# Two sums of a weight block made by an accumulating DMA, one more seven-product pair in gate/up, and the feed-forward stage in three parts

## The chip, the cores and the metric

The kernel runs on one core of one Trainium2 chip. A core has five engines that run their own instruction streams: TensorE (PE in the profile; PEld is its weight load), VectorE (DVE), ScalarE (ACT), GpSimd (POOL) and SyncE (SP, used here only to issue DMAs). Sixteen DMA engines move data between device memory (HBM) and the on-chip memory SBUF; PSUM holds the accumulators of TensorE. The metric is the device time of one execution in microseconds; smaller is better.

## The reference

A decoder trunk of two layers on 256 tokens of width 2048, in float32. Each layer has an input projection, three kinds of mixers in parallel, an output projection, and then the feed-forward stage (FFN), which this change is about:

```python
h = rms_norm(x, norm_ffn_w[l])
x = x + (jax.nn.silu(h @ ffn_w_gate[l]) * (h @ ffn_w_up[l])) @ ffn_w_down[l]
```

`ffn_w_gate` and `ffn_w_up` are 2048 x 5632, `ffn_w_down` is 5632 x 2048, for each of the two layers. The rest of the trunk is left as it is.

## The kernel before

**Precision.** Each float32 operand is split in a high part, rounded by ACT (`wh = Copy(raw)`, line 316), and a low part, made by DVE (`wl = raw - wh`, line 317). A product is then three matmuls into the same accumulator: high times high, low times high, high times low (line 1309, in `prod`).

**Tiles.** The FFN weights come in tiles `raw` of 128 x 1024, 512 KB, of which five are in flight (`RAW = 5`). Two tiles make a pair `kp`, which covers 256 rows of the contraction and two columns of 512: a 2 x 2 block of weights, against the 2 x 2 block of activations of the same 256 rows and the two halves of the 256 tokens. The layout of the weights in HBM is made beforehand (`_pairs`).

**Two kinds of pair.** A plain pair (kind `c`) does eight block products, 24 matmuls of 512 columns. A seven-product pair (kinds `s0`, `s1`, `s2`, in the manner of Strassen and Winograd) does seven, 21 matmuls, and has to make sums of blocks first. The sums of activations, four of 128 x 128, are made in `block_sums`: for gate/up on POOL, once a layer; for down on DVE, when a gate_up has ended, in `finish`. The sums of weights are made by DVE in `split`, lines 338 to 341: with raw = [a, b] of the first tile and r1 = [c, d] of the second, each 128 x 512, line 338 makes u1 = [a + d, b + d] in one instruction, line 340 a + d + b, line 341 that plus c, both in u2. Lines 344 and 345 split c; raw, u1 and u2 are then split as any tile. `SEVEN = (2, 4, 5)` names the seven-product pairs among the 8 of gate/up, `DOWN_SEVEN` six among the 22 of down.

**Loops.** `ffn` goes through the 11 column groups f of 512 in parts (`FFN_PARTS = [6, 5]`). In each part it calls `gate_up(f)` for each f, and then `down(g2)` for the two halves of the output columns, over the pairs 2f and 2f+1 of these f. `down` adds its result to the residual `res`: eight DVE adds around the seven-product terms (in `mid`) and four at the end. More parts mean more calls of `down`, and fewer activations held at a time. The very last group (layer 1, last part, second half) goes through `dense` and `final`, with plain tiles (`wdown`). What a gate_up leaves to be done late (its transposes, `finish`) is issued after the first pair of the next call (`flush`).

**Order and queues.** The code calls `wtile` for each part. It lets `fetch` issue loads so far that five tiles are loaded ahead of what has been split, on SP's DMA queue, and lets `split` run two parts ahead of TensorE (`SPLIT = 3` buffers). A framework turns the code into one instruction stream for each engine, may reorder instructions within a stream, and puts in the semaphore waits. Each stream then runs in order. The pool `up` has 22 buffers of 128 x 1040, for all working tiles `u`: activations, sums, and whatever else the stage holds.

Of the kernel before, what the change touches and what calls it, by code (L numbers as in the profile page):

```python
# [10 lines left out]
ALU = mybir.AluOpType  # L11
PSUM = bass.MemoryType.PSUM

P = 128
# [7 lines left out]
RWKV_EPS = 64e-5  # L22
EXP_HALF = math.exp(-0.5)

FFN_PARTS = [6, 5]

SEVEN = (2, 4, 5)

DOWN_SEVEN = (2, 5, 8, 14, 17, 19)

# [27 lines left out]
class Trunk:  # L60
# [194 lines left out]
    def plan(self):  # L255
        seq, parts, done = [], [], []

        def plain(tiles, kind="n"):
            for t in tiles:
                parts.append((kind, len(seq)))  # L260
                seq.append(t)
                done.append(len(seq))

        def pairs(w, first, kps, seven):
            for kp in kps:
                t = [(w, (first + 2 * kp + j) * P * 1024, 512) for j in range(2)]
                if kp in seven:
                    parts.extend((f"s{j}", len(seq)) for j in range(3))
                    seq.extend(t)
                    done.extend([len(seq)] * 3)  # L270
                else:
                    plain(t, "c")
        for l in range(DEPTH):
            off = 0
            for n in (IN_W[name] for name in IN_ORDER):
                plain((f"win{l}", off + kp * 2 * P * n, n) for kp in range(8))
                off += D * n
            for g in range(4):
                plain(("wout", (l * 4 + g) * D * 512 + kp * 2 * P * 512, 512) for kp in range(8))
            f0 = 0  # L280
            for nf in FFN_PARTS:
                for f in range(f0, f0 + nf):
                    pairs("wgu", (l * 11 + f) * 16, range(8), SEVEN)
                lastp = f0 + nf == 11
                for g2 in range(2):
                    if lastp and l + 1 == DEPTH and g2:
                        for g in range(2):
                            plain(("wdown", g * 2 * nf * 2 * P * 512 + kp * 2 * P * 512, 512) for kp in range(2 * nf))
                    else:
                        pairs("wdp", (l * 2 + g2) * 44, range(2 * f0, 2 * (f0 + nf)), DOWN_SEVEN)  # L290
                f0 += nf
        self.seq, self.parts, self.done = seq, parts, done
        self.loaded, self.cast, self.used = [], [], 0

    @staticmethod
    def cuts(i, n):
# [3 lines left out]
    def fetch(self, upto):  # L300
        while len(self.loaded) < min(upto, len(self.seq)):
            w, off, n = self.seq[len(self.loaded)]
            raw = self.wp.tile([P, 1024], F32, tag="raw", name=self.nm("raw"), bufs=self.RAW)
            src = self.A[w][off:off + 2 * P * n].rearrange("(p f) -> p f", p=P)
            for c in self.cuts(len(self.loaded), n):
                self.nc.sync.dma_start(raw[:, c], src[:, c])
            self.loaded.append(raw)

    def split(self, upto):
        nc = self.nc  # L310

        def halve(raw, cuts):
            wh = self.wp.tile([P, 1024], F32R, tag="wh", name=self.nm("wh"), bufs=self.SPLIT)
            wl = self.wp.tile([P, 1024], F32R, tag="wl", name=self.nm("wl"), bufs=self.SPLIT)
            for c in cuts:
                nc.scalar.activation(wh[:, c], raw[:, c], AF.Copy)  # L316
                nc.vector.tensor_tensor(wl[:, c], raw[:, c], wh[:, c].bitcast(F32), op=ALU.subtract)  # L317
            return wh, wl
        while len(self.cast) < min(upto, len(self.parts)):
            p = len(self.cast)  # L320
            kind, i = self.parts[p]
            raw = self.loaded[i]
            if kind == "n" and i >= len(self.seq) - 2 * FFN_PARTS[-1]:
                wh, wl = self.U(F32R), self.U(F32R)
                nc.scalar.activation(wh[:, :1024], raw, AF.Copy)
                nc.vector.tensor_tensor(wl[:, :1024], raw, wh[:, :1024].bitcast(F32), op=ALU.subtract)
                self.cast.append((wh, wl))
            elif kind == "n":
                self.cast.append(halve(raw, self.cuts(i, self.seq[i][2])))
            elif kind == "c":  # L330
                self.cast.append(halve(raw, [slice(0, 1024)]))
            elif kind == "s0":

                r1 = self.loaded[i + 1]
                u1, u2 = self.U(), self.U()
                h = lambda t, j: t[:, j * 512:(j + 1) * 512]
                v = lambda t: t[:, :1024].rearrange("p (a c) -> p a c", a=2)
                nc.vector.tensor_tensor(v(u1), v(raw), h(r1, 1).rearrange("p (o c) -> p o c", o=1).to_broadcast([P, 2, 512]),  # L338
                                        op=ALU.add)
                nc.vector.tensor_tensor(h(u2, 0), h(u1, 0), h(raw, 1), op=ALU.add)  # L340
                nc.vector.tensor_tensor(h(u2, 1), h(u2, 0), h(r1, 0), op=ALU.add)
                wh, wl = halve(raw, [slice(0, 1024)])
                b = self.U(F32R)
                nc.scalar.activation(h(b, 0), h(r1, 0), AF.Copy)
                nc.vector.tensor_tensor(h(b, 1), h(r1, 0), h(b, 0).bitcast(F32), op=ALU.subtract)
                self.cast.append((wh, wl, b))
                self.sums = (u1, u2)
                self.loaded[i + 1] = None
            else:
                self.cast.append(halve(self.sums[int(kind[1]) - 1][:, :1024], [slice(0, 1024)]))  # L350
            self.loaded[i] = None
# [81 lines left out]
    def post_pair(self, kp, src, scale, xh, xl):  # L433
# [10 lines left out]
        self.tt(fl(xl), w[:, :512], fl(xh).bitcast(F32), ALU.subtract)  # L444
        if kp in SEVEN:
            self.comb[kp] = self.block_sums(w, "pool")
# [905 lines left out]
    def gate_up(self, f, rstd):  # L1352
# [19 lines left out]
        def finish(t):  # L1372
            ps = self.PS()
            for k in range(4):
                self.tr(ps[:, k * P:(k + 1) * P], sg[:, t * 512 + k * P:t * 512 + (k + 1) * P], self.ident)
            o, p4 = hh[:, :, t * P:(t + 1) * P], ps.rearrange("p (k c) -> p k c", k=4)
            self.act(o, p4, AF.Copy)
            self.tt(hl[:, :, t * P:(t + 1) * P], p4, o.bitcast(F32), ALU.subtract)
            for b in need:

                self.act(need[b][:, 0:512].rearrange("p (k s c) -> p k s c", k=2, s=2)[:, :, t, :],
                         p4[:, 2 * b:2 * b + 2, :], AF.Copy)
                if t:
                    self.hcomb[2 * f + b] = self.block_sums(need[b], "dve")
        need = {b: self.U() for b in range(2) if 2 * f + b in DOWN_SEVEN}
        self.late += [lambda: finish(0), lambda: finish(1)]
        return hh, hl

    def ffn(self, l):
        f0 = 0  # L1390
        xt, rstd = self.xt, self.rstd
        for pi, nf in enumerate(FFN_PARTS):
            self.hcomb = {}
            hts = [self.gate_up(f, rstd) for f in range(f0, f0 + nf)]
            lastp = pi == len(FFN_PARTS) - 1

# [145 lines left out]
def _tiles(w, n):  # L1542

    k = w.shape[0] // (2 * P)
    return np.ascontiguousarray(w.reshape(k, 2, P, n).transpose(0, 2, 1, 3)).reshape(-1)


def _pairs(a, b, seven):

    k = a.shape[0] // (2 * P)  # L1550
    w = np.stack([a.reshape(k, 2, P, 512), b.reshape(k, 2, P, 512)], axis=2).transpose(0, 1, 3, 2, 4)
    o = np.empty((k, 2, P, 2, 512), w.dtype)
    for kp in range(k):
        if kp in seven:
            o[kp, 0, :, 0], o[kp, 0, :, 1], o[kp, 1, :, 0], o[kp, 1, :, 1] = \
                w[kp, 0, :, 0], w[kp, 1, :, 1], w[kp, 1, :, 0], w[kp, 0, :, 1]
        else:
            o[kp] = w[kp]
    return o.reshape(-1)


def _layout(i):
# [54 lines left out]
    for l in range(DEPTH):  # L1617
# [3 lines left out]
        wo += [_tiles(w[:, g * 512:(g + 1) * 512], 512) for g in range(4)]  # L1621
        gu += [_pairs(i["ffn_w_gate"][l][:, g * 512:(g + 1) * 512], i["ffn_w_up"][l][:, g * 512:(g + 1) * 512], SEVEN)
               for g in range(11)]
        d = [i["ffn_w_down"][l][:, g * 512:(g + 1) * 512] for g in range(4)]
        dp += [_pairs(d[2 * g], d[2 * g + 1], DOWN_SEVEN) for g in range(2)]
        if l + 1 == DEPTH:
            down += [_tiles(d[g][-512 * FFN_PARTS[-1]:], 512) for g in (2, 3)]
    o["wout"], o["wgu"], o["wdp"], o["wdown"] = (np.concatenate(x) for x in (wo, gu, dp, down))
# [23 lines left out]
```

## Time and profile before

| | us |
|---|---|
| median of 3 runs | 2401.75 (2401.61 to 2407.05) |
| profiled execution | 2401.77 |
| its span, first to last instruction | 2400.0 |
| DVE: first operation of a seven-product pair, line 338 | 106.1, 87 times |
| DVE: low parts from raw tiles, line 317 | 866.3, 720 times |
| DMA moved | 436.04 MB, mean 182 GB/s |

An "f period" below is the time between the same instruction in two gate_up calls that follow each other. A row of instructions by group has the line, the engine, the operation, out <- in, shapes and count, then the busy time and the mean duration in ns, and then the time that the engine idled before them and what ended it. A row of a timeline has the start, the duration, the engine, the line, the operation and in brackets the idle time before it. `u`, `raw`, `wh`, `wl`, `xh`, `xl`, `res` are tiles of the program; `dn` and `mx` are accumulators in PSUM.

### The profile page before, as it was taken

To read this page: it belongs to the slowest core of one execution; us is meant where nothing else is said; L and a number is where in the kernel's file an instruction comes from. 1 tells how busy PE (TensorE), PEld (TensorE's weight loads), DVE (VectorE), ACT (ScalarE), POOL (GpSimd) and SP (SyncE) were. 2 spreads that over 40 slices of the span, in tenths; PEclk is the share of its full clock that TensorE was granted. 3 is DMA by queue.
4 is the path that set the end of the run, shared out by engine and by line. 5 is a ranking of instruction groups with operands and counts; after the bars stand their busy time and mean duration, and the time that the engine had idled before them with its cause. 6 is when DMAs were issued, how large, how long until landed. Compare 5 with 4: busy or idle time off the path is not lost.

```text
span 2400.0 us, 34089 instructions
## 1 busy us (share of the span) xinstructions
PE 2374.5 (99%) x12947; PEld 1994.1 (83%) x12947; DVE 1874.1 (78%) x2439; ACT 1312.9 (55%) x1761; POOL 119.8 (5%) x149
## 2 busy tenths in 40 slices
PE   8999999999999999999999999999999999999998
PEld 8998888788888888778799988887878888887786
DVE  7777656589898788998867866565888987889884
ACT  6445755555555455555554547555555554555553
POOL 3100110100000000000001101101000000000000
PEclk9999999999999999999999999999999999999999
DMA  8464554555656565565644544545555565556654
GB/s 292 147 172 112 158 164 151 184 187 194 197 188 204 189 206 195 177 199 192 210 152 150 167 118 157 164 160 182 189 192 190 193 211 188 198 193 186 222 189 149
DMA packets 139429, 436.04 MB, mean 182 GB/s; under 512 B 30464, under 2 KB 30720, under 8 KB 139264
## 3 DMA queue, kind: packets, MB, share of 16 engines
q1 hardware_dynamic: 137360, 428.52, 55.2%
q0 software_dynamic: 1184, 4.19, 0.5%
q8 instruction: 101, 1.65, 0.3%
q10 hardware_dynamic: 720, 1.15, 0.2%
q14 instruction: 64, 0.52, 0.1%
HBM read 430.66 MB, written 3.15 MB: 181 GB/s over the span
## 4 chain that ended last, share of the span: by engine, by line
PE 87%; DVE 6%; ACT 3%; DMA 2%; issue 2%; POOL 0%; ACTq 0%; SPq 0%; POOLq 0%; DVEq 0%
PE dn L1309 41%; PE mx L1309 9%; PE dn L401 6%; PE dn L399 6%; PE dn L400 6%; PE dn L391 4%; PE dn L393 4%; PE dn L392 4%; PE mx L131 4%; DVE wl L317 2%; ACT wh L316 2%; PE mx L135 2%; DVE u L105 2%; ACT u L123 1%; DVE u L338 1%
## 5 line engine op out<-in xcount | busy, mean ns | idle before, releaser
L316 ACT ACTIVATE wh<-raw 128x1024 fp32r<-128x1024 f32 (+3 forms) x720 | 740.8, 1038 | 651.6 <-PE dn L1309 264.0
L317 DVE TENSOR_TENSOR wl<-raw,wh 128x1024 fp32r<-128x1024 f32 (+3 forms) x720 | 866.3, 1211 | 284.5 <-ACT wh L316 277.9
L1309 PE MATMUL dn<-wh,xh 128*128 128x512 f32 x946 | 372.0, 393 | 0.0
L1309 PE MATMUL dn<-wh,xl 128*128 128x512 f32 x946 | 368.9, 390 | 0.0
L1309 PE MATMUL dn<-wl,xh 128*128 128x512 f32 x946 | 365.0, 390 | 0.0
L1309 PE MATMUL dn<-wh,u 128*128 128x512 f32 x1128 | 352.4, 394 | 0.0
L316 ACT ACTIVATE wh<-u 128x1024 fp32r<-128x1024 f32 x174 | 184.7, 1062 | 215.2 <-PE dn L1309 100.3
L391 PE MATMUL dn<-xh,wh 128*128 128x256 f32 x896 | 258.3, 289 | 7.4 <-ACT wh L316 7.4
L393 PE MATMUL dn<-xh,wl 128*128 128x256 f32 x896 | 254.5, 286 | 1.2 <-DVE wl L317 1.1
L392 PE MATMUL dn<-xl,wh 128*128 128x256 f32 x896 | 255.0, 285 | 0.0
L317 DVE TENSOR_TENSOR wl<-u,wh 128x1024 fp32r<-128x1024 f32 x174 | 211.5, 1222 | 53.9 <-ACT wh L316 53.8
L1309 PEld LDWEIGHTS dn<-wh,u 128*128 128x128 f32 x1128 | 211.1, 188 | 48.1 <-DVE u L105 0.8
L1309 PE MATMUL dn<-wl,u 128*128 128x512 f32 x564 | 220.8, 394 | 0.1
L1309 PEld LDWEIGHTS dn<-wh,xh 128*128 128x128 f32 x946 | 177.6, 188 | 42.5 <-DVE u L105 3.9
L1309 PEld LDWEIGHTS dn<-wl,xh 128*128 128x128 f32 x946 | 177.6, 188 | 37.6
L1309 PEld LDWEIGHTS dn<-wh,xl 128*128 128x128 f32 x946 | 177.7, 188 | 35.9
L1309 PE MATMUL mx<-wh,u 128*128 128x512 f32 x564 | 180.8, 398 | 0.9
L391 PEld LDWEIGHTS dn<-xh,wh 128*128 128x128 f32 x896 | 173.4, 193 | 9.9 <-ACT wh L316 7.6
L393 PEld LDWEIGHTS dn<-xh,wl 128*128 128x128 f32 x896 | 172.9, 194 | 2.0 <-DVE wl L317 1.8
L392 PEld LDWEIGHTS dn<-xl,wh 128*128 128x128 f32 x896 | 173.5, 194 | 0.1
L399 PE MATMUL dn<-wh,xh 128*128 128x512 f32 (+2 forms) x448 | 170.4, 380 | 0.0
L401 PE MATMUL dn<-wl,xh 128*128 128x512 f32 (+2 forms) x448 | 162.4, 366 | 1.2 <-DVE wl L317 1.1
(179 smaller groups left out, 3482.9 us busy)
## 6 DMA issues: line engine op xcount, KB each, us to landing
raw<-wgu SPq DMA_DIRECT2D x352, 512.0 KB, 3.6
raw<-win SPq DMA_DIRECT2D x175, 512.0 KB, 4.0
raw<-wdp SPq DMA_DIRECT2D x156, 512.0 KB, 4.2
raw<-wout SPq DMA_DIRECT2D x64, 512.0 KB, 4.2
raw<-win SPq DMA_DIRECT2D x32, 340.0 KB, 3.0
raw<-wdown SPq DMA_DIRECT2D x20, 512.0 KB, 4.3
raw<-win SPq DMA_DIRECT2D x16, 360.0 KB, 3.1
u<-xt SPq DMA_DIRECT2D x8, 256.0 KB, 7.2
```

Source lines behind the costliest of these rows:

```text
L105: self.nc.vector.tensor_tensor(out, a, b, op=op)
L131: self.nc.tensor.matmul(out, lhsT=lhsT, rhs=rhs, start=start, stop=stop)
L135: self.nc.tensor.transpose(out, in_, ident)
L316: nc.scalar.activation(wh[:, c], raw[:, c], AF.Copy)
L317: nc.vector.tensor_tensor(wl[:, c], raw[:, c], wh[:, c].bitcast(F32), op=ALU.subtract)
L391: nc.tensor.matmul(o, lhsT=wh[:, c], rhs=xh, start=st and m % 2 == 0, stop=False)
L392: nc.tensor.matmul(o, lhsT=wh[:, c], rhs=xl, start=False, stop=False)
L393: nc.tensor.matmul(o, lhsT=wl[:, c], rhs=xh, start=False, stop=sp and m % 2 == 1)
L399: nc.tensor.matmul(o, lhsT=xh[:, x], rhs=wh[:, c], start=st, stop=False)
L400: nc.tensor.matmul(o, lhsT=xl[:, x], rhs=wh[:, c], start=False, stop=False)
L401: nc.tensor.matmul(o, lhsT=xh[:, x], rhs=wl[:, c], start=False, stop=sp)
L1309: mm(o, lhsT=x[a], rhs=w[b], start=start and i == 0, stop=stop and i == 2)
```

## The change

Line 338 goes. Instead, for each seven-product pair, `fetch` loads the first tile a second time, into a buffer u1 of the pool `up` (on SP's queue, right behind the load of the tile itself), and has POOL's DMA queue add the block d to both halves of u1: a DMA with an accumulating add, whose source is the block d in HBM, read twice. It is issued as soon as the second copy is there. `split` takes the finished u1 from `self.early`.

With that, pair 6 of gate/up becomes a seven-product pair (four of 8), down has five such pairs of 22 at other places, and the FFN is done in three parts of 4, 4 and 3 column groups instead of two of 6 and 5.

```diff
-FFN_PARTS = [6, 5]
-
-SEVEN = (2, 4, 5)
-
-DOWN_SEVEN = (2, 5, 8, 14, 17, 19)
+FFN_PARTS = [4, 4, 3]
+
+SEVEN = (2, 4, 5, 6)
+
+DOWN_SEVEN = (2, 5, 10, 13, 18)
...
+        self.summed, self.early = {i for kind, i in parts if kind == "s0"}, {}
...
             for c in self.cuts(len(self.loaded), n):
                 self.nc.sync.dma_start(raw[:, c], src[:, c])
+            if len(self.loaded) in self.summed:
+
+                u1 = self.U()
+                self.nc.sync.dma_start(u1[:, :1024], src)
+                b12 = self.A[w][off + 2 * P * n:off + 4 * P * n].rearrange("(p o f) -> p o f", p=P, o=2)[:, 1:2, :]
+                self.nc.gpsimd.dma_start(u1[:, :1024].rearrange("p (o f) -> p o f", o=2), b12.to_broadcast([P, 2, n]),
+                                         accum_op=ALU.add)
+                self.early[len(self.loaded)] = u1
             self.loaded.append(raw)
...
-                u1, u2 = self.U(), self.U()
+                u1, u2 = self.early.pop(i), self.U()
                 h = lambda t, j: t[:, j * 512:(j + 1) * 512]
-                v = lambda t: t[:, :1024].rearrange("p (a c) -> p a c", a=2)
-                nc.vector.tensor_tensor(v(u1), v(raw), h(r1, 1).rearrange("p (o c) -> p o c", o=1).to_broadcast([P, 2, 512]),
-                                        op=ALU.add)
                 nc.vector.tensor_tensor(h(u2, 0), h(u1, 0), h(raw, 1), op=ALU.add)
                 nc.vector.tensor_tensor(h(u2, 1), h(u2, 0), h(r1, 0), op=ALU.add)
```

## The prediction, made before the changed kernel was run

> **What bounds the kernel now.** I read the page's head and busy shares first, then the windows of the feed-forward stage (FFN), then single instructions in the timelines. Windows rows give the length, the busy time and instruction count of PE, PEld, DVE, ACT and POOL, the granted clock, the DMA share and GB/s.
>
> ```profile
> span 2400.0 us, 34089 instructions
> PE 2374.5 (99%) x12947; PEld 1994.1 (83%) x12947; DVE 1874.1 (78%) x2439; ACT 1312.9 (55%) x1761; POOL 119.8 (5%) x149
> PE 87%; DVE 6%; ACT 3%; DMA 2%; issue 2%; POOL 0%; ACTq 0%; SPq 0%; POOLq 0%; DVEq 0%
> ...
> 480.00:740.00 260.00, 259.51 (x1147) 209.32 (x1147) 232.46 (x271) 150.05 (x177) 1.61 (x1) 1.00 0.60 194
> 740.00:870.00 130.00, 130.00 (x567) 105.48 (x566) 100.32 (x107) 63.43 (x67) 0.00 (x0) 1.00 0.58 195
> ```
>
> TensorE sets the pace (99%, and 87% of the chain that ended last). 480 to 740 is six gate_up calls of layer 0, and there DVE is busy 232.5 of 260 us: 0.89. 740 to 870 is two down calls, DVE at 0.77. So gate/up is where DVE has least room. Next, what one matmul costs, and how long each gate_up takes. These are timeline rows (start, us, engine, line, operation): two matmuls 14 apart in a full stretch, and the DVE add that begins when the last matmul of a gate_up's first accumulator ends.
>
> ```profile
> 717.47 0.39 PE L1309 MATMUL dn<-wh,xh 128*128 128x512 f32 x1
> 720.64 0.39 PE L1309 MATMUL dn<-wl,xh 128*128 128x512 f32 x1
> ...
> 522.98 0.69 DVE L105 TENSOR_TENSOR u<-u,dn 128x512 f32<-128x512 f32 x1 [1.31 <-PE dn L1309]
> 565.71 0.69 DVE L105 TENSOR_TENSOR u<-u,dn 128x512 f32<-128x512 f32 x1 [1.31 <-PE dn L1309]
> 609.54 0.69 DVE L105 TENSOR_TENSOR u<-u,dn 128x512 f32<-128x512 f32 x1 [1.31 <-PE dn L1309]
> 653.36 0.69 DVE L105 TENSOR_TENSOR u<-u,dn 128x512 f32<-128x512 f32 x1 [1.31 <-PE dn L1309]
> 696.08 0.69 DVE L105 TENSOR_TENSOR u<-u,dn 128x512 f32<-128x512 f32 x1 [1.31 <-PE dn L1309]
> 739.95 0.69 DVE L105 TENSOR_TENSOR u<-u,dn 128x512 f32<-128x512 f32 x1 [1.31 <-PE dn L1309]
> ```
>
> One matmul costs 3.17 / 14 = 0.2264 us, not the 0.39 it is shown with (they overlap). A gate_up has 3 seven-product pairs of 21 matmuls and 5 plain pairs of 24: 183, or 41.4 us. The periods are 42.73, 43.83, 43.82, 42.72 and 43.87 us. The long ones are those of f = 2, 3 and 5, which follow f = 1, 2 and 4: just those whose outputs need block sums for down's pairs 2, 5 and 8, done on DVE at the start of the next f. So **1.1 us of TensorE is lost in each gate_up that carries such sums**. The place is the first seven-product pair (DVE rows, then two PE rows 15 matmuls apart):
>
> ```profile
> 707.45 1.02 DVE L105 TENSOR_TENSOR u<-u 128x128 f32<-128x128 f32 x4 [0.45 <-ACT u L123]
> 708.39 1.22 DVE L338 TENSOR_TENSOR u<-raw,raw 128x1024 f32<-128x1024 f32 x1
> 710.13 0.69 DVE L340 TENSOR_TENSOR u<-u,raw 128x512 f32<-128x512 f32 x1
> 710.82 1.22 DVE L317 TENSOR_TENSOR wl<-u,wh 128x1024 fp32r<-128x1024 f32 x1
> ...
> 710.92 0.39 PE L1309 MATMUL dn<-wl,u 128*128 128x512 f32 x1
> 715.17 0.39 PE L1309 MATMUL dn<-wh,xl 128*128 128x512 f32 x1
> ```
>
> Fifteen matmuls should take 3.40 us and took 4.25: the block sums push L338, L338 pushes the halves of u1 and u2, and TensorE gets those late.
>
> **The change, part by part.** All against the profiled execution: 2401.77 us (span 2400.0 and 1.77 around it), as good as the median of 2401.75.
>
> *Matmuls.* Pair 6 of gate/up becomes a seven-product pair: 11 x 2 = 22 more. Down goes from 21 such pairs (6 in layer 0's two calls each, 6 and 3 in layer 1) to 19 (10, 5 and 4; the last group, now 6 kps, stays plain). Net 20 pairs, 3 matmuls each: 60 x 0.2264 = **-13.6 us**. TensorE is the pace, so this counts in full as long as DVE and the DMAs keep up.
>
> *DVE.* The durations are the group rows (count | busy, mean ns):
>
> ```profile
> L338 DVE TENSOR_TENSOR u<-raw,raw 128x1024 f32<-128x1024 f32 x87 | 106.1, 1220 | 11.6 <-DMA raw<-wgu 6.0 <-DMA raw<-wdp 5.4
> L340 DVE TENSOR_TENSOR u<-u,raw 128x512 f32<-128x512 f32 x87 | 59.8, 688 | 1.1
> L317 DVE TENSOR_TENSOR wl<-u,wh 128x1024 fp32r<-128x1024 f32 x174 | 211.5, 1222 | 53.9 <-ACT wh L316 53.8
> ```
>
> A seven-product pair costs DVE 1.22 (L338) + 3 x 0.69 + 3 x 1.22 = 6.95 us and now 5.73; a plain one 2.44. A gate_up had 3 x 6.95 + 5 x 2.44 = 33.1 and gets 4 x 5.73 + 4 x 2.44 = 32.7 us. So DVE's sum hardly changes, while TensorE's falls by 0.68: L338's time is spent on the fourth pair. What does change is the order at pair 2: u1 no longer waits for DVE, and everything behind L338 moves up 1.22, more than the 1.1 lost there. There are 6 such gate_ups a layer: 12 x 1.1 = **-13.2 us**, if u1 is there in time. The other end is 0 (the stall stays because ACT's and the remaining DVE steps are as late). What ACT gets more with the new pair, one conversion of a whole tile and one of a half, lies beside TensorE: ACT is at 150 of 260 us.
>
> *Three parts.* Each layer gets two more down calls; the last group in layer 1 stays plain, so 7 calls become 11. Each has 12 DVE adds of 0.69 us: 33 us more DVE work, in a stage where DVE had 30 of 130 us free, beside the plain pairs. What a call loses now:
>
> ```profile
> 805.51 0.69 DVE L105 TENSOR_TENSOR res<-res,dn 128x512 f32<-128x512 f32 x1 [1.34 <-PE dn L1309]
> 870.14 0.69 DVE L105 TENSOR_TENSOR res<-res,dn 128x512 f32<-128x512 f32 x1 [1.34 <-PE dn L1309]
> ```
>
> 64.63 us for 3 x 21 + 9 x 24 = 279 matmuls, 63.17 us: 1.5 lost. If it goes with the call, 4 more cost +5.8; if it goes with L338, up to 7 x 1.5 = 10 are won. I take 0 between these ends: 19 pairs for 21, with less DVE work each. The plain tail has 6 tiles a group for 10, the same matmuls in all; 0.
>
> *DMA.* Every seven-product pair (107 now) loads its first tile twice and has 512 KB added to the second copy by POOL's queue, from a 256 KB block read twice. The rows: the start of the kernel, where queues are full; queue rows; landings of loads and of POOL's own DMAs; and where the loads are issued.
>
> ```profile
> 10.00:25.00 15.00, 13.60 (x105) 13.19 (x104) 11.55 (x16) 13.04 (x21) 5.24 (x3) 1.00 1.03 409
> ...
> q1 hardware_dynamic: 137360, 428.52, 55.2%
> raw<-wgu SPq DMA_DIRECT2D x352, 512.0 KB, 3.6
> u<-rg POOLq DMA_DIRECT2D x2, 512.0 KB, 6.5
> u<-rm POOLq DMA_DIRECT2D x2, 512.0 KB, 3.8
> u<-fnw POOLq DMA_DIRECT2D x2, 512.0 KB, 6.6
> ...
> 1160.22 0.54 POOL L250 DMA_DIRECT2D u<-rg  x1 [0.85 <-PE mx L1309]
> ...
> 702.12 2.67 SPq L306 DMA_DIRECT2D raw<-wgu  x2
> 710.88 2.73 SPq L306 DMA_DIRECT2D raw<-wgu  x2
> 719.54 0.68 DVE L340 TENSOR_TENSOR u<-u,raw 128x512 f32<-128x512 f32 x1
> 724.75 0.68 DVE L340 TENSOR_TENSOR u<-u,raw 128x512 f32<-128x512 f32 x1
> ```
>
> At 409 GB/s 512 KB hold all DMA engines 1.28 us. A gate_up then needs 16 + 4 loads, 25.6 us, and 4 accumulations, in about 42 us: it is DMA-bound only if one accumulation holds the engines over (42 - 25.6) / 4 = 4.1 us. No row shows an accumulation. The near end is a plain transfer, 1.28 us; the far end twice the slowest POOL landing, 13 us; I take 2.6, one transfer for reading the old sum and one for the new block, being nearer the plain transfers. That is 36 of 42 us. The Trainium skill (Collectives: The Full Stack, section "The bandwidth ceiling: the fold count and why AG ≠ RS ≠ AR") says that a reducing DMA runs at half a copy's rate, not because the addition costs but because two sources are read on one ring; by it an accumulation would be 2.56 us, an estimate, and the sum the same; no run here shows it yet.
>
> The latency is tighter. In the old trace pair 4's first tile is issued at 702.12 + 2.67 - 0.33 = 704.46 (one issue is 0.33 us), and its first sum is used by L340 at 719.54: 15.1 us ahead. For pair 5 it is 713.28 to 724.75: 11.5 us, and pair 6, which follows directly, will have about as much. The new chain in that time: tile and second copy land after 3.6 + 1.28 = 4.9 us; POOL, which waits for this, issues (0.55); the accumulation lands 3.8 to 6.6 us after its issue, and up to 1.28 later for the old sum's read: 9.3 to 13.3 us. Against 11.5: between 2.2 in hand and 1.8 late. DVE works in order, so an L340 that waits holds the halves of the plain tiles behind it; TensorE has up to two cast parts in stock and DVE one tenth of its time. I take 0.25 us of TensorE lost at each of pairs 5 and 6, 0.5 x 22 = **+11 us**; ends 0 and, at 1.8 late each with nothing absorbed, 3.6 x 22 = +79. The SP queue gets a wait for a free buffer ahead of each second copy; the raw loads behind it would be late too, and ACT and DVE with them. I price this at 0, as loads lead by over 11 us and land in 3.6. POOL does nothing else in gate/up (1.61 us in 260), so nothing there queues behind the new waits.
>
> Sum: 2401.8 - 13.6 - 13.2 + 11 = **2386 us**.
>
> **The rivals.**
>
> *The DMA keeps up.* The accumulation lands like rm (3.8): nothing late, 2401.8 - 26.8 = 2375, down to 2365 if down's stalls go as well. For it: 409 GB/s shown against some 300 needed. Chance 0.25 (2362 to 2378).
>
> *The accumulation comes late: slower.* If it lands 8.5 us after its issue, the chain is 4.9 + 0.55 + 8.5 = 14 us, 2.5 late at pairs 5 and 6. With half of that absorbed by DVE's slack and the stock, 1.25 x 2 x 22 = 55 us: 2375 + 55 = 2430. It decides from 26.8 / 22 = 1.2 us lost per gate_up, about 0.6 at each of the two pairs. For it: pairs 4, 5 and 6 follow each other, each asking 3 x 1.28 + 2.6 = 6.4 us of the DMA engines in 21 x 0.2264 = 4.75 us, so that the backlog grows by 1.7 us each, and the last is behind both. Against it: the lead of five tiles, and POOL rows no slower than 6.6. The Trainium skill (DMA: Bandwidth & Descriptors, section "Issuing engines are not separate DMA queues") says that DMAs of all issuers run on the same 16 engines, so POOL's queue brings no bandwidth of its own; that is this backlog. Chance 0.28.
>
> *The sums were not what TensorE waited for.* Then the 1.1 us stay with the block sums, only the matmuls go, and the same 11 us of lateness take nearly all of it: 2401.8 - 13.6 + 11 = 2399. For it: a DVE sum per gate_up that falls by only 0.4 us. Chance 0.14 (2395 to 2409).
>
> **How the numbers follow.** The forecast, 2378 to 2394, has 0.33. Faster by over 0.3% (7 us, about what a measurement of this kernel can tell from no change) is the forecast and the first rival, 0.58; within it the third, 0.14; slower 0.28. The range 2364 to 2436 leaves out the last microseconds of the good case and the worst of the late ones, where the far end of the accumulation's cost would lie.
>
> **What would show it.** Right: gate_up periods all near 42 us, long and short ones alike; L340 with little or no wait for the accumulation; about 60 fewer 512-column matmuls; POOL issues of about 0.6 us; a DMA share near 0.85 in gate/up. Wrong: L340 or ACT's conversion of u waiting on the accumulating DMA, longest at pairs 5 and 6; a landing over 7 us; SP waiting long for the second copy's buffer; down calls that each lose more than 1.5 us. The prediction falls if one accumulation holds the engines over 4 us, or if a stall at a new boundary between the three parts appears.

## The result, and the profile after

| | before | after |
|---|---|---|
| median, runs on the same chip | 2401.68 us (4 runs, 2399.99 to 2407.05) | 2540.64 us (4 runs, 2534.32 to 2542.64) |
| ratio, 95% interval | | 1.0577 [1.0562, 1.0591]: slower |
| profiled execution, its span | 2401.77, 2400.0 | 2539.19, 2536.9 |
| span less PE's busy time | 25.5 | 132.8 |
| mean granted TensorE clock | 0.997 | 0.977 |

The line numbers have moved: L313 is the new accumulating DMA, L311 the second copy, L307 the load of `raw`; L346 and L347 are the two additions into u2 (before L340, L341), L325 and L326 the high and low parts (L316, L317), L350 and L351 the halves of c, L1315 the matmuls.

The page of the changed kernel: its span, the busy shares, the DMA queues, the chain that ended last by engine, two groups, and DMA issues with the median time to landing.

```profile
span 2536.9 us, 34756 instructions
PE 2404.1 (95%) x12887; PEld 2009.4 (79%) x12887; DVE 1861.3 (73%) x2472; ACT 1345.7 (53%) x1801; POOL 250.9 (10%) x264
...
q1 hardware_dynamic: 152768, 484.62, 56.8%
q0 software_dynamic: 30288, 60.30, 13.2%
...
PE 71%; DMA 18%; DVE 5%; issue 2%; ACT 2%; POOL 1%; SPq 0%; DVEq 0%; POOLq 0%; ACTq 0%
...
L346 DVE TENSOR_TENSOR u<-u,raw 128x512 f32<-128x512 f32 x107 | 73.7, 688 | 180.0 <-DMA u<-wgu 142.1
L313 POOL DMA_DIRECT2D u<-wgu x88 | 106.2, 1221 | 959.6 <-DMA u<-wgu 323.1
...
raw<-wgu SPq DMA_DIRECT2D x352, 512.0 KB, 4.8
u<-wgu SPq DMA_DIRECT2D x88, 512.0 KB, 6.7
u<-wgu POOLq DMA_DIRECT2D x88, 512.0 KB, 8.5
```

The 60 matmuls are gone (12887 for 12947), and TensorE is nevertheless busy for 29.6 us more and idle for 107 us more. DMA's share of the last chain went from 2% to 18%. DVE's idle time before L346, 1.1 us in all before (L340), is 180 us, 142 of it ended by a DMA from the gate/up weights into u, which is the accumulation. Summed over the rows of DVE's timeline, 117 of the 180 us are pair 4's, which waits in every one of the 22 gate_ups; pairs 5 and 6 together have 31, down has 31 and pair 2 has 1. In the median a second copy lands 6.7 us after its issue, an accumulation 8.5 us.

The waits of the changed kernel (engine, operation and what it waited for: us in total, times, longest) show who else stands there:

```profile
DVE u L346 <- DMA u<-wgu: 142.1, 37, 8.3
ACT wh L325 <- DMA u<-wgu: 92.5, 16, 6.8
ACT u L350 <- DMA raw<-wgu: 55.9, 27, 4.1
```

Now one gate_up (f = 2 of layer 0). In its timeline come first SP's copies of pairs 4 and 5 and POOL's accumulations into them, then DVE's row order around pair 4.

```profile
592.96 0.86 SPq L311 DMA_DIRECT2D u<-wgu  x2
...
600.38 2.48 POOL L313 DMA_DIRECT2D u<-wgu  x2 [12.95 <-PE dn L1315]
...
602.83 2.35 DVE L326 TENSOR_TENSOR wl<-raw,wh 128x1024 fp32r<-128x1024 f32 x2
611.69 0.69 DVE L346 TENSOR_TENSOR u<-u,raw 128x512 f32<-128x512 f32 x1 [6.50 <-DMA u<-wgu]
612.30 1.22 DVE L326 TENSOR_TENSOR wl<-raw,wh 128x1024 fp32r<-128x1024 f32 x1
...
615.90 0.69 DVE L346 TENSOR_TENSOR u<-u,raw 128x512 f32<-128x512 f32 x1
621.12 0.69 DVE L346 TENSOR_TENSOR u<-u,raw 128x512 f32<-128x512 f32 x1
```

Two copies go out together, and two accumulations together. The copy of pair 4 leaves at 592.96 and lands 6.8 us later. POOL begins to issue at 600.38, 0.6 us behind that landing, and the accumulation lands 11.3 us after this, so that DVE begins the sum at 611.69: 18.7 us for the chain. DVE stands at L346 from 605.2 on, so the chain had 12.2. L346 of pairs 5 and 6 (the last two rows) then shows no wait; pair 5's accumulation took 14.2 us to land, and DVE, held up at pair 4, came to it just then. The low half made at 612.30 is that of pair 4's own first tile, and needs nothing of the accumulation; it stood behind L346 in DVE's order. (The matmul that it releases writes `mx`, into which only seven-product pairs are summed. In the gate_up before, the low half of a plain tile stood behind L346 as well.) The chain of the window goes through just this row, and the windows (busy time of PE, PEld, DVE, ACT and POOL, then clock, DMA share, GB/s) show what TensorE does meanwhile:

```profile
600.38 11.29 DMA u<-wgu
...
612.30 1.23 DVE wl L326
...
613.57 0.50 PE mx L1315
```

```profile
609.00:611.00 2.00, 0.40 (x2) 0.00 (x0) 0.00 (x0) 0.00 (x0) 0.31 (x1) 1.00 1.06 292
611.00:613.00 2.00, 0.00 (x0) 0.00 (x0) 1.31 (x2) 1.06 (x1) 0.89 (x1) 1.00 1.08 301
613.00:615.00 2.00, 1.43 (x6) 1.17 (x7) 2.00 (x4) 0.77 (x1) 0.00 (x0) 0.91 1.11 228
615.00:617.00 2.00, 2.00 (x6) 1.63 (x5) 1.95 (x3) 1.76 (x3) 0.00 (x0) 0.50 1.12 243
617.00:619.00 2.00, 2.00 (x8) 1.54 (x8) 2.00 (x3) 0.79 (x1) 0.00 (x0) 0.74 1.01 398
619.00:621.00 2.00, 2.00 (x10) 1.64 (x9) 2.00 (x3) 1.62 (x3) 0.00 (x0) 1.00 0.42 102
```

TensorE ends its stock at 609.4 and begins again at 613.57, 4.2 us later. Then its granted clock falls to 0.50 and 0.74 for two windows of 2 us: 1.0 + 0.5 us more, and 0.2 in the window before. Together that is 5.9 us. The period of this gate_up is read from the same additions in two of them:

```profile
584.62 1.37 DVE L105 TENSOR_TENSOR u<-u,dn 128x512 f32<-128x512 f32 x2
632.92 1.37 DVE L105 TENSOR_TENSOR u<-u,dn 128x512 f32<-128x512 f32 x2
```

It is 48.3 us, 6.0 more than the 42.3 of a kernel without the accumulations (e2, below). So a gap of 4 us costs about 6. The Trainium skill (TensorE: Matmul & The Clock Gate, section "What's actually happening") says that the clock drops to half after an idle window of about 3.4 us and comes back after as long a busy one; the trace agrees, with 0.50 behind a gap of 4.2 us, and the full clock again by 619.

### The profile page after: what moved, and what is told of

It is laid out like the page before. It is cut to its first block, busy times and chain, and to the rows that moved or that the text cites. A ratio compares the mean times of both kernels' runs of the same rounds, so it can differ in the third digit from the quotient of the medians.

```text
span 2536.9 us, 34756 instructions
## 1 busy us (share of the span) xinstructions
PE 2404.1 (95%) x12887; PEld 2009.4 (79%) x12887; DVE 1861.3 (73%) x2472; ACT 1345.7 (53%) x1801; POOL 250.9 (10%) x264
## 3 DMA queue, kind: packets, MB, share of 16 engines
q0 software_dynamic: 30288, 60.30, 13.2%
## 4 chain that ended last, share of the span: by engine, by line
PE 71%; DMA 18%; DVE 5%; issue 2%; ACT 2%; POOL 1%; SPq 0%; DVEq 0%; POOLq 0%; ACTq 0%
PE dn L1315 28%; DMA u<-wgu 13%; PE mx L1315 8%; PE dn L407 6%; PE dn L405 6%; PE dn L406 6%; PE dn L397 4%; PE dn L399 4%; PE dn L398 4%; DVE wl L326 4%; PE mx L131 3%; DMA u<-wdp 3%; DMA raw<-wgu 2%; PE mx L135 2%; ACT u L123 1%
## 5 line engine op out<-in xcount | busy, mean ns | idle before, releaser
L325 ACT ACTIVATE wh<-raw 128x1024 fp32r<-128x1024 f32 (+3 forms) x704 | 725.6, 1037 | 612.7 <-PE dn L1315 208.8
L326 DVE TENSOR_TENSOR wl<-raw,wh 128x1024 fp32r<-128x1024 f32 (+3 forms) x704 | 845.4, 1213 | 262.8 <-ACT wh L325 259.6
L325 ACT ACTIVATE wh<-u 128x1024 fp32r<-128x1024 f32 x214 | 226.5, 1059 | 328.1 <-PE dn L1315 129.8
L1315 PE MATMUL dn<-wh,u 128*128 128x512 f32 x1260 | 395.2, 397 | 0.0
L1315 PE MATMUL dn<-wl,xh 128*128 128x512 f32 x792 | 313.2, 401 | 46.2 <-DVE wl L326 46.2
L326 DVE TENSOR_TENSOR wl<-u,wh 128x1024 fp32r<-128x1024 f32 x214 | 259.9, 1221 | 76.8 <-ACT wh L325 75.8
L1315 PE MATMUL dn<-wh,xh 128*128 128x512 f32 x792 | 316.0, 399 | 0.0
L1315 PE MATMUL dn<-wh,xl 128*128 128x512 f32 x792 | 314.2, 397 | 0.0
L1315 PEld LDWEIGHTS dn<-wh,u 128*128 128x128 f32 x1260 | 238.5, 190 | 53.8 <-DVE res L105 0.7
L1315 PE MATMUL dn<-wl,u 128*128 128x512 f32 x630 | 248.3, 398 | 11.5 <-DVE wl L326 11.5
L1315 PE MATMUL mx<-wh,u 128*128 128x512 f32 x680 | 219.8, 405 | 0.0
L1315 PEld LDWEIGHTS dn<-wl,xh 128*128 128x128 f32 x792 | 151.9, 193 | 84.5 <-DVE wl L326 52.4
L346 DVE TENSOR_TENSOR u<-u,raw 128x512 f32<-128x512 f32 x107 | 73.7, 688 | 180.0 <-DMA u<-wgu 142.1
L313 POOL DMA_DIRECT2D u<-wgu x88 | 106.2, 1221 | 959.6 <-DMA u<-wgu 323.1
L1315 PEld LDWEIGHTS dn<-wh,xh 128*128 128x128 f32 x792 | 152.1, 192 | 32.5 <-ACT wh L325 1.8
L1315 PEld LDWEIGHTS dn<-wh,xl 128*128 128x128 f32 x792 | 152.0, 192 | 32.2
```

What stands on the lines that cost most here:

```text
L313: self.nc.gpsimd.dma_start(u1[:, :1024].rearrange("p (o f) -> p o f", o=2), b12.to_broadcast([P, 2, n]), accum_op=ALU.add)
L1315: mm(o, lhsT=x[a], rhs=w[b], start=start and i == 0, stop=stop and i == 2)
```

## The experiments

A time with a ratio is the median of 4 to 10 executions, and a time without one is a single execution. The kernel before, run beside them, gave 2398.5 to 2401.1 us. Edits are to the changed kernel.

**e1: the sums back on DVE**, everything else of the change kept.

```diff
-            if len(self.loaded) in self.summed:
...
-                self.early[len(self.loaded)] = u1
...
+                nc.vector.tensor_tensor(v(u1), v(raw), h(r1, 1).rearrange("p (o c) -> p o c", o=1).to_broadcast([P, 2, 512]),
+                                        op=ALU.add)
```

> The changed kernel with the first two sums back on DVE: no second copy, no accumulation; four pairs of 8, five of 22 and three parts stay. Theory A (the loss is all in the accumulated sums coming late by DMA): the 60 matmuls are saved, DVE is fuller by 1.2 us at each pair, so 2385 to 2410 us, TensorE idle about 25 us as before, granted clock 0.997. Rival C (the fourth pair or the third part costs it): stays above 2450 us, with DVE as what TensorE waits for.

2413.22 us, ratio 1.0065 [1.0048, 1.0081]. The window of e1 over gate_ups of layer 0:

```profile
480.00:680.00 200.00, 196.23 (x852) 154.13 (x851) 188.75 (x224) 119.05 (x143) 3.99 (x5) 1.00 0.58 186
```

That is 3 us above theory A's range and well below rival C's. DVE is busy 188.75 of 200 us and TensorE no longer all the time. A fourth seven-product pair on DVE alone loses more than its matmuls bring: e16 (below), which differs from e1 in this pair alone, took 2397.14 us. Of the +139, all but 12 to 15 us belongs to how the sums are made.

**e2: the second copy alone**, no accumulation (the block d is left out of the sums).

```diff
...
-                self.nc.gpsimd.dma_start(u1[:, :1024].rearrange("p (o f) -> p o f", o=2), b12.to_broadcast([P, 2, n]),
-                                         accum_op=ALU.add)
```

> The changed kernel with the second copy of the tile, without the accumulating DMA (the addition of the fourth block to the first two sums is left out). Theory A1 (the accumulations fill the DMA engines just where three pairs follow each other): 20 loads of 1.28 us per gate_up fit, no wait of L346 over 1 us, 2360 to 2385 us. Rival A2 (the extra bytes as such are too many): a good part of the waits stays, above 2430 us.

2378.33 us. Nothing waits for u, and the periods are 42.4, 42.3 and 42.3 us: the stall of 1.1 us is gone, though the copies are there (60.8% of the DMA engines' time in q1 for 55.2%). So neither the copies nor the rest of the change cost the time. POOL's accumulation does, with the wait for it: 162 us.

**e3: POOL's DMA writes and doesn't add.** (The diff takes `accum_op=ALU.add` away.)

> The changed kernel with POOL's DMA writing the block over the second copy instead of adding to it (the addition is left out): same chain copy, POOL, DMA; same blocks and packets of 2 KB; no read of the old sum. Theory A1 (the adding itself holds the engines, 3.0 us per transfer by the queue's share against 1.3 to 1.5 for a plain one): POOL's queue falls from 13 to 6 or 7% of the engines' span, the waits of L346 fall by over half, 2400 to 2450 us. Rival B (the serial chain of copy, issue by POOL and landing): it falls little, above 2500 us.

2451.51 us, just above theory A1's range. The page and the waits:

```profile
q0 software_dynamic: 16592, 60.30, 7.2%
...
u<-wgu POOLq DMA_DIRECT2D x88, 512.0 KB, 6.0
```

```profile
DVE u L345 <- DMA u<-wgu: 73.9, 30, 6.2
```

An accumulation takes (13.2% x 2536.9 - 12 of plain transfers) / 107 = 3.0 us of all 16 engines, the same write without addition (7.2% x 2449.2 - 12) / 107 = 1.5: a factor of 2. The Trainium skill (Collectives: The Full Stack, section "The bandwidth ceiling: the fold count and why AG ≠ RS ≠ AR"), quoted in the prediction, has this factor for the reducing step of a collective; here the trace shows it for an accumulation into SBUF. POOL's issue is 0.72 us here and 1.22 with the addition. Even a plain write at this place comes late and costs 73 us over e2.

**e4: rows of 4 KB.** SP writes d twice, and POOL adds the whole tile, to see whether the short rows of the accumulation (2 KB) make it slow.

```diff
-                self.nc.sync.dma_start(u1[:, :1024], src)
...
+                self.nc.sync.dma_start(u1[:, :1024].rearrange("p (o f) -> p o f", o=2), b12.to_broadcast([P, 2, n]))
+                self.nc.gpsimd.dma_start(u1[:, :1024], src, accum_op=ALU.add)
```

> The changed kernel with the two transfers exchanged: SP's queue writes the fourth block twice, POOL's DMA adds the whole tile to it, in rows of 4 KB instead of 2 KB; the sums are the same. Rival D (what is slow is the packets of 2 KB): POOL's queue falls from 13 to about 7% of the span and the time below 2470 us. Theory A1 (each added byte costs, whatever the packet): the share stays over 11% and the time within 40 us of 2540.

2533.37 us, q0 at 12.7%, landing 7.7. The size of the rows is not the cause.

**e5 and e6: the accumulation (or a plain write) into a buffer that nobody reads.** The sums then lack d; the pool `up` has 21 buffers.

```diff
...
+                self.nc.gpsimd.dma_start(self.spare.rearrange("p (o f) -> p o f", o=2), b12.to_broadcast([P, 2, n]), accum_op=ALU.add)
```

> The changed kernel, but POOL's accumulating DMA of each pair goes to a spare buffer that nothing reads (the fourth block is left out of the sums; up has 21 buffers instead of 22): the same second copy and the same added bytes, of which nothing waits for the accumulation. Theory A1 (the engines' time: the accumulations hold the loads up): raw and second copies land late, 2440 to 2520 us. Rival B (the serial chain of copy, POOL's issue and landing is too long for its lead): no more than 15 us over the run with the copy alone, so 2375 to 2395 us.

> As the run before, with a plain write instead of the addition into the spare buffer. Theory A1: the run with the plain write in the chain (2451 us) lost 73 us to bytes, so 2420 to 2450 here. Rival B: 2375 to 2390, the 73 us were the chain's length.

2684.78 and 2540.42 us; neither run answers the question. Without a dependency the framework moved these DMAs ahead, the first to 2 us after the start, into the input projection and the mixers, where POOL has work of its own that queued behind them. The waits of e5 show the transfers one behind the other:

```profile
POOL spare L315 <- DMA spare<-wgu: 480.9, 85, 10.0
```

**e9: the same, held in its place** by a small copy on POOL from u1 into the spare buffer ahead of each accumulation.

```diff
+                self.nc.gpsimd.tensor_copy(self.spare[:, 0:128], u1[:, 0:128])
```

> As e5 (accumulation into a spare buffer that nothing else reads, the fourth block left out of the sums), but a small copy on POOL, from the second copy to the spare buffer, stands ahead of each accumulation, so that it can't be issued before the second copy is there: the same bytes in the same places as in the changed kernel, with nothing waiting for the accumulation. By e7 I now hold both: A1 as far as e7's rest goes (engines full, loads late), B for what e7 won. Both: 2400 to 2450 us. B alone: within 15 us of the run with the copy alone (2378). A1 alone: over 2480.

2408.73 us: 30 above e2. So the accumulations' work on the engines, with nobody waiting for their result, costs 30 us; the waits of e9 say through whom (ACT for raw tiles):

```profile
ACT u L353 <- DMA raw<-wgu: 75.5, 40, 4.6
```

Here one accumulation ended before the next began, so contention in the changed kernel may be somewhat more. The other 130 us need the waiting.

**e7 and e10: more lead.** Copy and accumulation of a pair are issued three tiles earlier; in e10 also without the addition.

```diff
-            if len(self.loaded) in self.summed:
+            k = len(self.loaded) + 3
+            if k in self.summed:
...
+                w, off, n = self.seq[k]
```

> The changed kernel with the second copy and the accumulation issued three tiles earlier (with the load of the tile three before the pair's first); the same work, sums complete. Rival B: 7 to 8 us more lead, against waits of L346 of 5 to 8 us, so the waits nearly vanish: 2380 to 2410 us. Theory A1: the transfers of pairs 4, 5 and 6 still meet, only earlier; half or more of the loss stays, above 2450 us.

> e7 (three tiles earlier) with a plain write instead of the addition (the addition is left out). If the 68 us that e7 still loses to the copy alone are the engines' time for reading the old sums, they nearly go: 2380 to 2400 us. If they are the second transfer as such: above 2420.

2446.49 and 2390.71 us. In e7 both theories hold in part: three tiles win back 94 of the 162 us, and DVE's waits for the accumulation are gone. What is left in e7 are raw loads that come late for ACT and DVE:

```profile
ACT u L353 <- DMA raw<-wgu: 118.9, 50, 4.8
DVE u L349 <- DMA raw<-wgu: 38.0, 19, 4.3
```

With plain writes (e10) it is only 12 above e2. So of the 68 us that e7 still loses, 56 go with the addition, and its accumulations take the engines twice as long (q0 14.0% for 7.4%).

**e8: the sums on POOL itself**, by its own addition.

> The changed kernel with the first two sums made by POOL from the tiles (one addition of 128x1024, some 2 to 2.5 us), no second copy and no accumulation. If DVE's 1.22 us per pair is what held the version with DVE's sum at 2413 us and POOL is on time, 2380 to 2395 us, faster than before; if POOL's reads slow DVE down or POOL is late, 2400 us or more.

2560.38 us, ratio 1.0675 [1.0657, 1.0693]. The groups of e8:

```profile
L318 DVE TENSOR_TENSOR wl<-raw,wh 128x1024 fp32r<-128x1024 f32 (+3 forms) x704 | 910.5, 1304 | 235.7 <-ACT wh L317 233.5
L339 POOL TENSOR_TENSOR u<-raw,raw 128x1024 f32<-128x1024 f32 x107 | 286.6, 2679 | 1188.0 <-DMA raw<-wgu 687.5 <-DMA raw<-wdp 341.3 <-DVE wl L318 79.6
L342 DVE TENSOR_TENSOR u<-u,raw 128x512 f32<-128x512 f32 x107 | 97.1, 907 | 0.8
```

POOL needs 2679 ns for what DVE did in 1220, and DVE's own operations beside it get slower in the mean of the run (1304 ns for 1213, 907 for 688).

**Which pairs are late?** By theory M only accumulations that run side by side are late; by theory L each one with the short lead is. First two pairs by DMA three tiles early (e11) and pair 2 alone without extra lead (e12); the others, and down's, on DVE:

```diff
+        self.summed = {i for kind, i in parts if kind == "s0" and seq[i][0] == "wgu"
+                       and seq[i][1] // (P * 1024) % 16 // 2 in (2,)}
```

> The changed kernel with the sums by DMA for pairs 2 and 5 of gate/up alone, three tiles earlier; pairs 4 and 6 and down's have theirs from DVE. If half the accumulations fit beside the loads, and half of L338's time is enough relief for DVE: 2380 to 2400 us, no wait for an accumulation over 1 us. If DMA or DVE still binds: 2405 or more.

> The same for pair 2 alone, with the changed kernel's own timing (no earlier issue); in the changed kernel pair 2 hardly waited, as no other accumulation is near it. The sum at pair 2 comes in time: 2390 to 2408 us, DVE holding what is left over 2380. If even a lone accumulation is late: 2415 or more.

2398.34 us, ratio 0.9993 [0.9981, 1.0005], and 2400.4 us, 1.0003 [0.9991, 1.0014]. In e12 the accumulation lands after 8.1 us, hardly sooner than in the changed kernel (8.5), and hardly anybody waits for it: pair 2 stands behind the plain pairs 0 and 1 and the change of f, and DVE comes to the sum 14 to 27 us after the copy's issue. It takes 13 us off e1.

Then the seven-product pairs at other places, all by DMA: SEVEN = (2, 4, 5) in e13, (2, 4, 6), which are not neighbours, in e14.

> The changed kernel with SEVEN = (2, 4, 5): three accumulations per gate_up instead of four, pairs 4 and 5 still neighbours, all sums of gate/up and down by DMA. Theory M (the accumulations are late because they meet: pairs 4, 5 and 6 in one stretch, each then landing after 11 to 14 us): with two that meet the loss falls to about half, 2440 to 2490 us. Theory L (a lone chain of copy, POOL's issue and accumulation is already as long as its lead): the loss per accumulation stays, so about three quarters of it, 2500 us or more.

> The same with SEVEN = (2, 4, 6), so that no two such pairs are neighbours: the same number of transfers and bytes as in e13. Theory M: nothing meets, 2400 to 2430 us, and no wait for an accumulation over 3 us. Theory L: as e13, within 20 us of it.

2461.32 and 2507.32 us. Theory M expected little waiting in e14, and that fell: the issue order put the copies of pairs 4 and 6 side by side there too, and L346 of pair 4 waits 6.1, 4.5 and 3.0 us in three gate_ups in a row. Theory L's 20 us fell as well: e14 is 46 us above e13. DVE's idle time before L346 differs by nearly as much, 146.9 us in e14 for 104.5 in e13, and the chain at pair 4 takes 16.3 us for 13.6 in the median. What makes it longer was not settled.

So pair 4 alone (e17) and pair 5 alone (e18), without extra lead, in the kernel with four pairs:

> The changed kernel with the half-sum of pair 4 of gate/up alone made by the accumulating DMA, with no earlier issue; the other three pairs there and the five of down add on DVE. Pair 4 has about 12 us from the issue of its copy to the moment its sum is wanted. Theory L (each accumulation with the short lead of the second half is late by itself): DVE waits 2 us or more for it in each gate_up, 22 x 2 = 44 us above the kernel with pair 2 alone (2400): 2420 to 2450. Theory M (only accumulations and copies that run side by side are late): the copy lands in about 5 us and the accumulation in about 8, together with the issue no more than 14 us, so at most 1 to 2 us of wait and a time of 2398 to 2415.

> The same with pair 5 alone by the accumulating DMA. Its lead by the estimate before the change was 11.5 us, the shortest of the four. Theory L: a wait of 2 us or more in each gate_up, 2420 to 2450. Theory M: a wait under 2 us, 2398 to 2415. If pair 4 waits and pair 5 doesn't, the lead is set by where POOL's issue stands behind the product before and not by the order of the pairs.

2471.03 and 2415.6 us, with e12 at 2400. The pages of e17 and e18, then DVE's waits for the accumulation in each:

```profile
span 2469.3 us, 34320 instructions
PE 2399.0 (97%) x12887; PEld 1990.7 (81%) x12887; DVE 1949.5 (79%) x2557; ACT 1344.2 (54%) x1801; POOL 151.1 (6%) x179
```

```profile
span 2413.7 us, 34328 instructions
PE 2372.4 (98%) x12887; PEld 1982.6 (82%) x12887; DVE 1949.1 (81%) x2557; ACT 1345.3 (56%) x1801; POOL 154.2 (6%) x179
```

```profile
DVE u L353 <- DMA u<-wgu: 66.2, 18, 8.6
```

```profile
DVE u L353 <- DMA u<-wgu: 19.2, 6, 4.1
```

For pair 4 theory L holds, with a loss above its range: one lone accumulation a gate_up comes late. Its timeline (copy, POOL's issue, sum used):

```profile
633.34 2.44 SPq L313 DMA_DIRECT2D u<-wgu  x1
640.58 1.19 POOL L315 DMA_DIRECT2D u<-wgu  x1 [46.69 <-PE mx L1322]
648.94 0.69 DVE L353 TENSOR_TENSOR u<-u,raw 128x512 f32<-128x512 f32 x1 [4.46 <-DMA u<-wgu]
```

15.6 us from the copy's issue to the sum, of which 11.1 were to be had; in the gate_up before it was 13.5 with 12.9 to be had, a wait of only 0.6. Pair 5 lies between the theories: of 22 gate_ups only six wait. What decides is the lead, the time from the copy's issue until DVE is at the sum. The chain is nearly the same, 13.8 us in the median of e17 and 14.1 in e18, and in 20 of the 22 gate_ups of each POOL begins 0.5 to 0.6 us behind the copy's landing. But at pair 4 the lead is 9.1 to 12.9 us in 18 of 22 gate_ups; at pair 5 it is 10.4 to 10.6 us in the six that wait, and 15.6 or more in the others. And 66 us of waiting cost 71, 19 us cost 15: in e17 TensorE's idle time (span less busy) is 70.3 us for 41.3 in e18, and its busy time 26.6 higher at the same matmuls, with a mean clock of 0.988 for 0.996. Meeting makes it worse still, 17.2 us in the median at pair 4 of the changed kernel for 13.8 alone, but it isn't needed for the loss.

**A version of both: e15**, three parts, SEVEN = (2, 4, 5), pair 2's sum by DMA two tiles early, the rest on DVE; and **e16**, the same with every sum on DVE.

> SEVEN = (2, 4, 5) as in the kernel before, three parts, sums by DVE except those of pair 2 of gate/up, which come by DMA, issued two tiles earlier. A lone accumulation lands 8.1 us after its issue (e12), which the lead now covers; the 1.1 us that TensorE lost at pair 2 after each f with block sums (10 f now) should go: 2385 to 2396 us, faster than before. If that stall has another cause, 2398 to 2408 us.

> The same with all sums by DVE: the kernel before but for the three parts and the five places in down. If the third part costs nothing: 2400 to 2403 us (two seven-product pairs fewer are 6 matmuls, 1.4 us more; two stalls of 1.1 us fewer). If it costs the 1.5 us lost per call of down, four times: 2405 to 2408 us.

e15: 2388.9 us, ratio 0.9957 [0.9942, 0.9973], faster than the changed kernel, and 0.4% faster than the kernel before. e16: 2397.14, 0.9991 [0.9979, 1.0003], 3 us under its range. The DVE rows that end a first accumulator, of e15 and then of e16:

```profile
520.99 0.69 DVE L105 TENSOR_TENSOR u<-u,dn 128x512 f32<-128x512 f32 x1 [1.31 <-PE dn L1324]
563.72 0.69 DVE L105 TENSOR_TENSOR u<-u,dn 128x512 f32<-128x512 f32 x1 [1.31 <-PE dn L1324]
606.81 0.69 DVE L105 TENSOR_TENSOR u<-u,dn 128x512 f32<-128x512 f32 x1 [1.31 <-PE dn L1324]
```

```profile
521.83 0.69 DVE L105 TENSOR_TENSOR u<-u,dn 128x512 f32<-128x512 f32 x1 [1.31 <-PE dn L1310]
564.56 0.69 DVE L105 TENSOR_TENSOR u<-u,dn 128x512 f32<-128x512 f32 x1 [1.31 <-PE dn L1310]
608.43 0.69 DVE L105 TENSOR_TENSOR u<-u,dn 128x512 f32<-128x512 f32 x1 [1.31 <-PE dn L1310]
```

The second period is 43.09 us with the DMA and 43.87 without. Ten gate_ups have such a long period in each run, and ten times 0.78 are 7.8 of the 8.2 us between the two.

## Why the prediction was wrong

Foretold were 2386 us, in a range that ended at 2436; it became 2541. By its steps:

- **Matmuls, -13.6: right in number**, 60, but worth less: the short periods of 42.7 us came down to 42.3 in e2, 0.4 us for the 0.68 of three matmuls. Why was not settled. **The stall, -13.2: its cause was right**, its size nearly: in e2 the long periods are near 42.3 too, and from e16 to e15, where DVE loses only L338's work at pair 2, the step wins 0.78 of the 1.1 us a long gate_up. Both terms together were -26.8, and e2, where they stand without the accumulation, is 20 us below the kernel before.
- **DVE's sum and the three parts: right.** With the fourth pair's sums on DVE it is busy 94% of gate/up (e1), and the parts with down's new places make no difference that can be measured (e16).
- **The engines' time of an accumulation: nearly right**, 3.0 us for 2.6, and a DMA share of 0.88 in two gate_ups (540 to 620 us) for 0.85 foretold. The price put on loads that come late by it, 0, was wrong: some 30 us (e9), more in e7.
- **The latency: here the prediction failed**, in the term "+11 us". Its chain was 4.9 us for the copy, 0.55 for POOL's issue and 3.8 to 6.6, up to 1.28 more, for the landing: 9.3 to 13.3. The trace has 6.7 us for the copy and 8.5 for the landing in the median, and at pair 4, where the loss is, the whole chain took 17.2 us, alone (e17) 13.8. The two landings are the links that were too short: they came from rows of DMAs at a lighter load and without an addition. The middle link came out, by luck: 0.55 us was the length of an issue, and POOL does begin 0.56 us behind the copy's landing, but its issue with the addition then takes 1.22 us, which is part of the 8.5.
- **The lead: wrong at pair 4.** 15.1 us were read off the old trace, up to L340 at 719.54. The rows of DVE ahead of it there are these (the first is of pair 3's two tiles):

```profile
715.00 2.35 DVE L317 TENSOR_TENSOR wl<-raw,wh 128x1024 fp32r<-128x1024 f32 x2
717.27 1.22 DVE L338 TENSOR_TENSOR u<-raw,raw 128x1024 f32<-128x1024 f32 x1
718.41 1.22 DVE L317 TENSOR_TENSOR wl<-raw,wh 128x1024 fp32r<-128x1024 f32 x1
```

The change takes L338 out, and in the new order the sum stands ahead of the low half at 718.41, which is that of pair 4's first tile. Without these two, DVE would have been at the sum at 717.35, 12.9 us after the tile's issue, where the prediction, counting on 15.1, put no loss. In the changed kernel it was there 9.0 to 12.3 us after the copy's issue in 18 of 22 gate_ups, and in e17, where DVE still makes the other pairs' sums, after 9.1 to 12.9. So the loss came at pair 4, not mainly at 5 and 6. DVE mostly waited 5 to 8 us there, and TensorE lost 5.9 us in the gate_up shown, not 0.25 at each of two pairs. Pair 5 then has time: while DVE stands at pair 4 its accumulation lands.

- **What a wait costs.** "Half of that absorbed" was assumed in the rival that came nearest (2430, chain 14 us): right in its mechanism, short in its size, and at pairs 5 and 6 instead of 4. In the gate_up shown 6.5 us of waiting were 4.2 us for TensorE, and the clock behind such a gap put some 1.7 on top. The clock stood in no step. Over the whole run, against e2 with the same matmuls, TensorE is idle for 106 us more and busy for 54 more. An estimate from the mean granted clocks (0.977 over 2536.9 us, 0.998 over 2376.6) gives some 54 us for the clock, so that about a third of the loss is the slower clock behind the gaps.

Open: what lengthens the chain in e14 against e13, and how far the 30 us of e9 hold where accumulations overlap.

## What to carry to other kernels

A chain of dependent transfers (copy, then accumulate) is to be priced by its landing times under the load that the change itself makes, link by link, and set against the time until an in-order engine reaches its use, read for each place in the order that the change leaves, without the work that it takes out. If the chain is longer, the engine waits at the head of its queue and holds up work that needs nothing of it; where the gap on TensorE came to about 4 us, the clock added 1.7 us of its own. Move one sum with a long lead (here pair 2's) rather than all: e15, which does this, beat the kernel before by 0.4%, and e16, which does not, did not differ from it.

## What was not expected of the hardware

- An accumulating DMA of 512 KB took 3.0 us of all 16 engines for 1.5 of the same plain write, POOL's issue 1.22 us for 0.72, and in e12, with the only accumulation of a gate_up, it still landed 8.1 us after its issue. Rows of 4 KB took 12.7% of the engines' time for 13.2% with rows of 2 KB (e4).
- While accumulations run the engines are full at some 300 GB/s (the windows from 609 to 613 us above), where the start of the kernel reached 409 with plain loads.
- With POOL's own additions beside them, DVE's operations took 7% (L318) and 32% (L342) longer in the mean of the run (e8).
